# A decoder block in split float32: the slots of the 4 KB tiles made 64 bytes longer

## The chip, the cores and the metric

The kernel runs on one core of one Trainium2 chip. The metric is the device time of one execution in microseconds (us), the median over several runs. Three runs of the kernel before gave 1765.37, 1765.73 and 1765.88 us, so the median is 1765.73 us.

## The reference

One decoder block works on 256 tokens of width 2048 in float32:

```
u    = rmsnorm(x)
proj = u @ w_in                       # 2048 x 16896: HGRN2 q,f,i,gate | attention q,k,v | two merge gates
ya   = hgrn2(...)  @ w_proj_a         # 16 heads of 128, gated linear recurrence
yb   = dilated_attention(...) @ w_proj_b   # 3 groups of 4 heads
mix  = sigmoid(gate_a) * ya + sigmoid(gate_b) * yb
h    = x + mix @ w_out
v    = rmsnorm(h)
hc   = causal_conv3(v @ w_up) + conv_b     # 2048 x 11264
h    = h + (gelu(hc[:, :5632]) * hc[:, 5632:]) @ w_down
out  = rmsnorm(h)
```

Nearly all of the arithmetic lies in the products with the weight matrices. All inputs and outputs are float32.

## The kernel before, in words

**Arithmetic.** The kernel multiplies float32 numbers with the faster float32r matmuls of the TensorE. Each operand is split into a part `hi` (the float32r rounding) and a part `lo` (the rest), and a product is the sum of three matmuls: hi by hi, hi by lo, lo by hi. The weights are split on the chip: ACT writes `hi` (L248), DVE writes `lo` (L249).

**The stream of weights.** All weight matrices are laid out beforehand as one stream of 300 units of 16 tiles (128 x 128). The SP queue loads each unit (1 MB) into a `raw` tile. `split(u)` turns it into two `hi` and two `lo` tiles of 4 KB per partition each, and `next_tiles(n)` (L282) hands out the next n weight tiles of 128 columns. Three units ahead are loaded and two are split. These tiles lie in the pool `wp`, which has three slots of 8 KB for `raw` and four slots of 4 KB each for `hi` and `lo`.

**The two kinds of product step.** `moving_step` (L381) uses four weight tiles as the moving operand of 512 columns. Its stationary operand is a piece of 128 columns of the activations, `xl` or `xh`. It issues three matmuls for each of two token halves: L386 (`xl` by `hi`), L387 (`xh` by `hi`) and L388 (`xh` by `lo`). The stage of the feed-forward block, both merge gates, the two projections and the output product run this way. Counted from the loops there are 976 such steps, so 1952 matmuls at each of the three lines, 5856 in all. `tile_step` (L296) does it the other way round: one weight tile is stationary, and the activations are the moving operand. L299 takes `hi` by 512 columns (both parts of the activations), L300 takes `lo` by 256 columns. There are 56 x 16 = 896 such pairs, for the columns that are wanted transposed.

**Weight loads.** Every matmul is preceded by its own load of the stationary operand (the rows LDWEIGHTS, engine PEld). The load for the next matmul runs beside the matmul before it.

**Tiles and slots.** Almost every other large tile comes from `w4` (L158): 28 slots of 4096 bytes per partition, in the pool `sb`. The split activations `xu`, `hv`, `mix`, `ob`, `ot` and `ff` are `w4` tiles, and so are the inputs, the gates and the state of the recurrence. The pools lie behind each other in the order `const`, `wp`, `sb`, and `w4` is the first tag of `sb`. The slots of `wp` add up to a multiple of 512 bytes, so every `hi`, `lo` and `w4` slot begins at the same place of its 512 bytes, and every piece of 128 columns (512 bytes) does too. In this text the **phase** of an operand is its start minus the start of the `hi` tiles, modulo 512 bytes; it is 0 for all of these. A few smaller tiles have another phase, which follows from the sizes of the tiles in their order, each slot rounded up to 32 bytes: `ones_r` (in `const`, used at L556 and L557) has 416, the tag `o2` with the tiles `ks` (L577) has 384 (twelve slots of 32 bytes lie ahead of it), and `a01` (the `a` of L612) has 320. The tile `z` (L601) is a `w4` tile with phase 0.

**Order of the work.** The products of the weight stream set the order on the TensorE. The recurrence and the attention are written as generators, from which `pump` (L265) takes steps, so their small float32 matmuls and transposes stand between the products (L475 to L632). In the feed-forward block the transposes at L797 do.

Of the kernel before, what the change touches and what calls it, by code (L numbers as in the profile page):

```python
# [13 lines left out]
U8 = mybir.dt.uint8  # L14
# [4 lines left out]
P = 128  # L19
# [128 lines left out]
def hybrid_block(ctx, tc, x_p, x_t, weights, g1, gf, params, c_rope, c_mask0, c_mask1, c_level, out):  # L148
# [5 lines left out]
    sb = ctx.enter_context(tc.tile_pool(name="sb", bufs=1))  # L154
# [1 line left out]
    pss = ctx.enter_context(tc.tile_pool(name="pss", bufs=4, space=bass.MemoryType.PSUM))  # L156

    def w4(shape, name, dt=F32):  # L158
        return sb.tile([P] + list(shape), dt, tag="w4", name=name, bufs=28)

    def w1(name, n=T, dt=F32):
        return sb.tile([P, n], dt, tag="w1", name=name, bufs=12)
# [29 lines left out]
    def in_turn(*instructions):  # L192

        with ExitStack() as stack:
            for i in instructions:
                stack.enter_context(tc.issue_after(i.ins))
            yield

    xt = [w4([4, T], f"xt{q}") for q in range(4)]

    def load_x(k0, k1):
# [19 lines left out]


    xu = [w4([2, 2, T], f"xu{i}", F32R) for i in range(KD // 2)]

    def x_pair(k):
# [114 lines left out]
    def first_norm():  # L340
        for q in range(4):
            sq = w4([4, T], f"sq{q}")
            act.activation(sq, xt[q], AF.Square)
            r = w1("ssqp", T) if q else ssq
            vec.tensor_reduce(r, sq.rearrange("p k t -> p t k"), axis=AX.X, op=ALU.add)
            if q:
                vec.tensor_tensor(ssq, ssq, r, op=ALU.add)
            yield 1.7
        rsqrt_rows(ssq, D, rstd, "rstd1")
        yield 4.0  # L350
        for i in range(2):
            vec.tensor_tensor(rope[:, i], rope[:, i], rstd, op=ALU.mult)
        ps = side_bank("rt")
        for m in range(2):
            pe.transpose(ps[:, m * P : (m + 1) * P], rstd[:, m * P : (m + 1) * P], ident)
        for m in range(2):
            vec.tensor_copy(rst[:, m : m + 1], ps[:, m * P : m * P + 1])
        with in_turn(*last):
            lower_bounds()
        yield 2.0  # L360
# [305 lines left out]
    for g in range(NGRP):  # L666
        z = four(f"z{g}", True)
        f = w4([2, HG, P], f"f{g}")
# [19 lines left out]
    for n in range(2):  # L688
        for j in range(NJ):
            t = w4([2, 512], f"eg{n}_{j}")  # L690
# [46 lines left out]
    for j in range(NJ):  # L737
        t = w4([2, 512], f"h{j}")
# [23 lines left out]
    for j in range(NJ):  # L762
# [4 lines left out]
        for i in range(2):  # L767
            pt = side_bank(f"ht{j}_{i}").rearrange("p (c t) -> p c t", c=2)
            for c in range(2):
                for m in range(2):  # L770
                    n = (2 * i + c) * P
# [123 lines left out]
```

## Time and profile before

| what | value |
|---|---|
| median of three runs | 1765.73 us |
| the profiled execution, its own time | 1768.19 us |
| its span, from first to last instruction | 1766.4 us |
| granted TensorE clock | 0.998 |
| PE busy | 1749.9 us (99%), 8472 matmuls |
| PEld (weight loads) busy | 1463.5 us (83%) |
| DVE busy | 1092.5 us (62%) |
| ACT busy | 888.6 us (50%) |
| read from HBM | 321.41 MB |

PE rows are matmuls. [...] In a timeline row the columns are start, duration, engine, line, operation, out<-in by tile names, and shape. In a row that names a single group, `x352` is the count, and three numbers behind a colon are the shortest, median and longest duration in ns; in rows with a bar, the numbers are the busy time in us and the mean of one in ns, and then the idle time before.

### The profile page before, as it was taken

The page shows a single profiled execution, that of the slowest core. Times are in us where ns is not written, and L with a number is a line of the kernel's source. Part 1 is how long each engine was busy: PE and PEld are TensorE (multiplying, and loading weights), DVE is VectorE, ACT ScalarE, POOL GpSimd, SP SyncE. Part 2 cuts the span into 40 slices and gives each one's busy share as a digit, 9 for nine tenths or more (in the row PEclk, how much of TensorE's full clock was granted, in tenths as well). Part 3 has the DMA queues.
Part 4 walks back from the last instruction along what each step waited for, and adds up shares of the span by engine and source line. Part 5 has one row for each costly group of instructions (what it writes and reads, how often), then busy time and mean ns, then how long its engine had stood idle before and what let it go on. Part 6 is the DMA issues. An engine that isn't in the chain of part 4 may idle for free.

```text
span 1766.4 us, 21297 instructions
## 1 busy us (share of the span) xinstructions
PE 1749.9 (99%) x8472; PEld 1463.5 (83%) x8472; DVE 1092.5 (62%) x1295; ACT 888.6 (50%) x1084; POOL 9.4 (1%) x24
## 2 busy tenths in 40 slices
PE   9999999999999999999999999999999999999997
PEld 7888888888888888888888888888888888888885
DVE  7765575777768675445565556666664456666654
ACT  6444465545454555444445455555543345555442
POOL 0000000000000000000000000000000000000000
PEclk9999999999999999999999999999999999999999
DMA  7665634544444444555556555455555554555552
GB/s 274 220 209 201 228 143 145 179 165 179 167 167 167 166 168 167 191 190 191 191 185 227 185 191 185 177 186 191 182 189 196 196 188 176 184 215 185 188 197 98
DMA packets 48371, 328.02 MB, mean 186 GB/s; under 512 B 5600, under 2 KB 5856, under 8 KB 10128
## 3 DMA queue, kind: packets, MB, share of 16 engines
q1 hardware_dynamic: 45648, 318.28, 50.7%
q0 software_dynamic: 1472, 5.24, 1.1%
q10 hardware_dynamic: 1152, 3.15, 0.5%
q8 instruction: 66, 1.08, 0.2%
q14 instruction: 33, 0.27, 0.0%
HBM read 321.41 MB, written 2.10 MB: 183 GB/s over the span
## 4 chain that ended last, share of the span: by engine, by line
PE 97%; DVE 1%; DMA 1%; ACT 0%; issue 0%; SPq 0%; DVEq 0%; ACTq 0%
PE ub L387 5%; PE ub L386 5%; PE ub L388 5%; PE ua L387 5%; PE ua L388 5%; PE ua L386 5%; PE dn L387 5%; PE dn L386 5%; PE dn L388 5%; PE egp L388 3%; PE egp L386 3%; PE egp L387 3%; PE ak L299 3%; PE aq L299 2%; PE wo L388 2%; PE gp L387 2%
## 5 line engine op out<-in xcount | busy, mean ns | idle before, releaser
L249 DVE TENSOR_TENSOR lo<-raw,hi 128x1024 fp32r<-128x1024 f32 (+1 forms) x602 | 734.5, 1221 | 575.5 <-ACT hi L248 565.9
L248 ACT ACTIVATE hi<-raw 128x1024 fp32r<-128x1024 f32 (+1 forms) x602 | 636.0, 1057 | 763.3 <-PE dn L387 127.3
L387 PE MATMUL ub<-hi,hv 128*128 128x512 f32 x352 | 139.2, 395 | 0.0
L387 PE MATMUL ua<-hi,hv 128*128 128x512 f32 x352 | 138.8, 394 | 0.0
L387 PE MATMUL dn<-hi,ff 128*128 128x512 f32 x352 | 137.4, 390 | 0.0
L386 PE MATMUL ub<-hi,hv 128*128 128x512 f32 x352 | 137.3, 390 | 0.0
L386 PE MATMUL ua<-hi,hv 128*128 128x512 f32 x352 | 137.3, 390 | 0.0
L388 PE MATMUL ub<-lo,hv 128*128 128x512 f32 x352 | 137.2, 390 | 0.0
L388 PE MATMUL ua<-lo,hv 128*128 128x512 f32 x352 | 137.2, 390 | 0.0
L386 PE MATMUL dn<-hi,ff 128*128 128x512 f32 x352 | 137.1, 390 | 0.0
L388 PE MATMUL dn<-lo,ff 128*128 128x512 f32 x352 | 137.1, 389 | 0.0
L386 PE MATMUL egp<-hi,xu 128*128 128x512 f32 x256 | 100.7, 393 | 0.0
L388 PE MATMUL egp<-lo,xu 128*128 128x512 f32 x256 | 99.9, 390 | 0.0
L387 PE MATMUL egp<-hi,xu 128*128 128x512 f32 x256 | 99.8, 390 | 0.0
L386 PEld LDWEIGHTS ub<-hi,hv 128*128 128x128 f32 x352 | 66.1, 188 | 14.0
L386 PEld LDWEIGHTS dn<-hi,ff 128*128 128x128 f32 x352 | 66.1, 188 | 13.8
L386 PEld LDWEIGHTS ua<-hi,hv 128*128 128x128 f32 x352 | 66.1, 188 | 13.8
L388 PEld LDWEIGHTS dn<-lo,ff 128*128 128x128 f32 x352 | 66.1, 188 | 13.6
L387 PEld LDWEIGHTS dn<-hi,ff 128*128 128x128 f32 x352 | 66.1, 188 | 13.5
L388 PEld LDWEIGHTS ua<-lo,hv 128*128 128x128 f32 x352 | 66.2, 188 | 13.1
L387 PEld LDWEIGHTS ua<-hi,hv 128*128 128x128 f32 x352 | 66.2, 188 | 13.0
L388 PEld LDWEIGHTS ub<-lo,hv 128*128 128x128 f32 x352 | 66.2, 188 | 13.0
(435 smaller groups left out, 3154.9 us busy)
## 6 DMA issues: line engine op xcount, KB each, us to landing
raw<-weights SPq DMA_DIRECT2D x298, 1024.0 KB, 4.8
h<-x_t ACTq DMA_DIRECT2D x4, 512.0 KB, 7.5
xt<-x_p SPq DMA_DIRECT2D x3, 512.0 KB, 10.3
xs_q<-aqraw POOLq DMA_DIRECT2D x6, 256.0 KB, 6.8
xs_k<-akraw POOLq DMA_DIRECT2D x6, 256.0 KB, 7.2
raw<-weights SPq DMA_DIRECT2D x4, 256.0 KB, 4.8
raw<-weights SPq DMA_DIRECT2D x2, 512.0 KB, 8.1
gfb<-gf POOLq DMA_DIRECT2D x2, 512.0 KB, 6.6
```

The source lines that it names most:

```text
L248: last[0] = act.activation(hi[:, q * w : (q + 1) * w], raw, AF.Copy)
L249: last[1] = vec.tensor_tensor(lo[:, q * w : (q + 1) * w], raw, hi[:, q * w : (q + 1) * w].bitcast(F32), op=ALU.subtract)
L299: pe.matmul(ps, hi, pair, start=(k == 0), stop=False, skip_group_check=True)
L386: pe.matmul(pst[m], xl, hi, start=(k == k0), stop=False)
L387: pe.matmul(pst[m], xh, hi, start=False, stop=False)
L388: pe.matmul(pst[m], xh, lo, start=False, stop=(k == k0 + nk - 1))
```

## The change

Only the helper `w4` differs. It takes a tile of 4160 bytes per partition, whatever the shape asked for, and returns a view of its first bytes in that shape:

```diff
     def w4(shape, name, dt=F32):
-        return sb.tile([P] + list(shape), dt, tag="w4", name=name, bufs=28)
+
+        n = math.prod(shape)
+        t = sb.tile([P, (4096 + 64) // (1 if dt == U8 else 4)], dt, tag="w4", name=name, bufs=28)[:, :n]
+        names = "abcd"[: len(shape)]
+        return t.rearrange(f"p ({' '.join(names)}) -> p {' '.join(names)}", **dict(zip(names, shape)))
```

Slot number s of `w4` now begins 64 x s bytes later than before, so its phase is 64 x s modulo 512: one slot in eight keeps phase 0, the others take 64, 128, 192, 256, 320, 384 and 448. The slots of `wp` and `const` stay where they are. The 28 slots take 1792 bytes more per partition, so the tags behind `w4` move on by 1792 bytes, which is 256 modulo 512 (`ks` goes from phase 384 to 128). The instructions, their shapes, their order and the waits that the program states are the same.

## Prediction

> **What bounds the kernel now.** I read the page first: the span, the busy times, and the chain that ended last.
>
> ```profile
> span 1766.4 us, 21297 instructions
> PE 1749.9 (99%) x8472; PEld 1463.5 (83%) x8472; DVE 1092.5 (62%) x1295; ACT 888.6 (50%) x1084; POOL 9.4 (1%) x24
> PEclk9999999999999999999999999999999999999999
> PE 97%; DVE 1%; DMA 1%; ACT 0%; issue 0%; SPq 0%; DVEq 0%; ACTq 0%
> ```
>
> The chain is matmuls for 97% of the span, at full clock. Nothing else ends last anywhere that matters, so the time is the number of matmuls times the distance between their starts, and only a change of that distance can move it. The profiled execution took 1768.19 us, 1.8 us more than its span and 2.5 us more than the median of the runs; I add my differences to the median.
>
> Next I took the timeline of a quiet stretch, in the output product, to see that distance.
>
> ```profile
> 1000.50 0.39 PE L387 MATMUL wo<-hi,mix 128*128 128x512 f32 x1
> 1000.73 0.39 PE L388 MATMUL wo<-lo,mix 128*128 128x512 f32 x1
> 1000.73 0.19 PEld L386 LDWEIGHTS wo<-hi,mix 128*128 128x128 f32 x1
> 1000.95 0.39 PE L386 MATMUL wo<-hi,mix 128*128 128x512 f32 x1
> ...
> 1001.86 0.39 PE L387 MATMUL wo<-hi,mix 128*128 128x512 f32 x1
> ```
>
> From 1000.50 to 1001.86 there are six distances, so one is 1.36 / 6 = 0.227 us. The load of the next weights starts with the matmul and lasts 0.19 us, so it lies beside the matmul that streams. The 5856 matmuls of the moving steps cost about 5856 x 0.227 = 1329 us of the span. The pairs of the tile steps look like this:
>
> ```profile
> 121.78 0.40 PE L299 MATMUL ak<-xu,hi 128*128 128x512 f32 x1
> 122.01 0.28 PE L300 MATMUL ak<-xu,lo 128*128 128x256 f32 x1
> ...
> 123.19 0.40 PE L386 MATMUL avp<-hi,xu 128*128 128x512 f32 x1
> ```
>
> Four pairs fit between 121.78 and 123.19, so a pair takes 0.353 us, and the 896 pairs take 316 us.
>
> **What the change can touch.** It adds no instruction, no wait and no byte of transfer. It moves the start of operands. Two reads run together on the TensorE: the moving operand of one matmul and the weights of the next. Before, both begin at phase 0 in every product; after, the activations have phases of 64 x s. The question is what a matmul loses when the weights beside it are read from another phase. The trace of before holds a few such cases, and one where no weights are read beside the matmul at all. The latter is the first matmul of a block, when the transposes behind it wait for ACT.
>
> ```profile
> 1035.31 0.39 PE L386 MATMUL ub<-hi,hv 128*128 128x512 f32 x1
> 1035.57 0.20 PEld L797 LDWEIGHTS ua0t<-ident,ua0u 128*128 128x128 f32 x2 [0.30 <-ACT ua0u L789]
> ...
> L386 PE MATMUL ub<-hi,hv 128*128 128x512 f32 x1 | 0.4, 388 | 0.0
> ...
> L386 PE MATMUL ub<-hi,hv x352: 388/389/398, 1035.3 to 1643.7; 128*128 128x512 f32 x176
> ```
>
> The matmul at 1035.31 has the array to itself: the next load starts 0.26 us later, past the 0.227 us that a matmul takes of the stream. Its duration is 388 ns. The median of its line, with weights of phase 0 read beside it, is 389 ns. So in the kernel before, the load beside the matmul costs 1 ns, 1.5 at most. **This is what there is to win** by taking the two reads apart: 5856 x 1.5 x 7/8 (one slot in eight keeps its phase) = 7.7 us. The shortest duration anywhere gives a wider bound:
>
> ```profile
> L387 PE MATMUL egp<-hi,xu x256: 386/389/398, 623.0 to 808.5; 128*128 128x512 f32 x128
> ```
>
> With 386 in place of 389 and a half for all, the gain would be 3.5 x 7/8 x 5856 = 17.9 us. I take this as the lower end.
>
> The side work gives the cost of other phases. In each of the next groups the line with PEld shows which weights were read beside the matmul of the product, and the row with the bar gives that matmul's own duration. The first is phase 0 (`z`), then 320 (`a`), 384 (`ks`) and 416 (`ones_r`).
>
> ```profile
> 684.46 0.19 PEld L601 LDWEIGHTS lv<-qp,z 128*128 128x128 f32 x1
> ...
> L388 PE MATMUL egp<-lo,xu 128*128 128x512 f32 x1 | 0.4, 388 | 0.0
> ```
> ```profile
> 697.62 0.19 PEld L612 LDWEIGHTS ho<-v,a 128*128 128x128 f32 x1
> ...
> L388 PE MATMUL egp<-lo,xu 128*128 128x512 f32 x1 | 0.4, 389 | 0.0
> ```
> ```profile
> 678.08 0.19 PEld L577 LDWEIGHTS lv<-qp,ks 128*128 128x128 f32 x1
> ...
> L388 PE MATMUL egp<-lo,xu 128*128 128x512 f32 x1 | 0.4, 396 | 0.0
> ```
> ```profile
> 628.20 0.19 PEld L556 LDWEIGHTS dg<-pr,ones_r 128*128 128x128 f32 x1
> ...
> L388 PE MATMUL egp<-lo,xu 128*128 128x512 f32 x1 | 0.4, 397 | 0.0
> ```
>
> Phases 0 and 320 leave the matmul at 388 and 389 ns. Phases 384 and 416 lengthen it to 396 and 397 ns, though the load itself keeps its 0.19 us. The reader is to see that a phase other than 0 never made a matmul shorter by more than the 1 ns, and that some phases cost 7 ns. `z`, `a` and `ks` are plain float32 weights and `ones_r` is float32r, like the products; the kind of number is thus not what divides them.
>
> **The sum.** For the moving steps I take the eight phases as equally frequent. Phase 0 costs nothing, by definition. 320 has its own row, 389 against a mean of 389 or 390 in the lines of the products: I take -1 ns, the most that it can be. 384 has +7 ns. 448 has no row; its nearest is 416, so +7. 64, 128, 192 and 256 have none; 64 lies next to 0, 256 next to 320, and the other two between them, so I take 0 for all four. The sum is (-1 + 7 + 7) / 8 = 1.62 ns per matmul, or 5856 x 1.62 = 9.5 us. The bounds: if the four unknown phases cost 7 ns too, it is (6 x 7 - 1) / 8 = 5.1 ns, or 30 us; if all seven gain, it is the -7.7 or -17.9 us from above.
>
> For the tile steps the roles are turned: the weights stay at phase 0 and the moving operand goes to 64 x s. The same side loads beside them show nothing dearer:
>
> ```profile
> 528.77 0.19 PEld L557 LDWEIGHTS dg<-pr,ones_r 128*128 128x128 f32 x1
> ...
> L299 PE MATMUL z3p<-xu,hi 128*128 128x512 f32 x2 | 0.7, 392 | 0.0
> ...
> L299 PE MATMUL aq<-xu,hi x128: 390/398/404, 78.0 to 167.2; 128*128 128x512 f32 x128
> ```
>
> The two matmuls there have a mean of 392 ns, where the median of the line is 398. The spread of that line, 390 to 404, shows that pairs do wander; 896 times 6 ns either way is 5 us, which both ends of the range can hold. I take 0.
>
> The rest of the change costs nothing, because it is hidden. ACT and DVE read and write `w4` tiles at new phases, but they are busy for 50% and 62%; if each of their instructions took 1% longer, DVE would be busy for 11 us more under a TensorE at 99%, and if that cover were gone, these 11 us would be the price. The loads of the input into `w4` slots are the same bytes in the same pieces. Where the matmuls grow by some ns nothing else becomes late, since all other engines wait for the TensorE.
>
> So the forecast is 1765.73 + 9.5 = **1775.2 us**, slower by 0.5%.
>
> **The rivals.** *The phase does not matter* (this includes that the slots would not really be moved to new phases, for instance by a rounding of their length to 512 bytes). Then the distances stay at 0.227 and 0.353 us and the time at 1765.7, within 3.5 us. For it speaks that a weight load costs a matmul 1 ns before, and that all 512-byte pieces of all slots give the same 389. Against it speak the 396 and 397 ns. In this kernel the two reads would have to be independent of each other. [...]
>
> *The matmuls become shorter.* The reads would collide at phase 0 for the whole of a load, and be free of each other at most of the others. It decides from the point at which the mean over the slots falls below the 389 of now. Taking away what the load costs gives 1765.7 - 7.7 = 1758 us, the shortest duration for all gives 1748. For it speaks that the four phases from 64 to 256 are unseen; against it, that the matmul without any load beside it is no shorter than 388. [...]
>
> *Every unseen phase costs what 384 costs*, or the disturbance of one matmul carries over to the next ones. This gives 1796 us, and is the upper end of the forecast and no case of its own.
>
> **How the numbers follow.** About 0.2%, or 3.5 us, is what a measurement of this kernel can tell from no change. Two rows of four phases show a cost and none a gain, so slower has the larger chance, 0.50. That the phase does not matter, or that costs and small gains cancel, has 0.27. Shorter matmuls have 0.23, because half of the phases are unseen and their mean decides the sign. The range is 1750 to 1796 us: the lower end is the gain by the shortest duration rounded inwards, the upper end the 30 us. If it is slower, the range of that case alone is 1769 to 1796.
>
> **What would show it right or wrong.** In the profile after, the instructions stay at 21297 and the loads at 0.19 us. If I am right, the groups of L386 to L388 split by tile: pieces in slots of phase 384 and 448 have medians near 396, those of 0 and 320 stay at 389, and the distance in a quiet stretch is 0.227 us in some stretches and 0.232 to 0.234 in others. If the phase does not matter, every one of these groups has the median of before. If the groups fall to 386 or below and the distance to 0.224 us or less, the collision was real and I am wrong on the sign. A median that is the same for all phases, but higher than before, would say that the cost is in the change from slot to slot and not in the phase.

## The result, and the profile after

The changed kernel takes 1787.55 us (median of four runs, 1787.22 to 1787.87), the kernel before beside it 1765.81 us (1765.37 to 1766.58). The ratio is 1.0123, 95% interval 1.0105 to 1.0140: slower by 21.7 us. The forecast was slower by 9.5 us, with a range from 1750 to 1796.

The page of the changed kernel has the same rows as before. Its lines are four higher in number, so L390, L391 and L392 are L386, L387 and L388 of before.

```profile
span 1785.5 us, 21297 instructions
PE 1770.2 (99%) x8472; PEld 1465.7 (82%) x8472; DVE 1093.3 (61%) x1295; ACT 888.2 (50%) x1084; POOL 9.4 (1%) x24
PEclk9999999999999999999999999999999999999998
PE 98%; DVE 1%; DMA 0%; SPq 0%; ACT 0%; issue 0%; DVEq 0%
L253 DVE TENSOR_TENSOR lo<-raw,hi 128x1024 fp32r<-128x1024 f32 (+1 forms) x602 | 734.3, 1221 | 594.0 <-ACT hi L252 584.7
L252 ACT ACTIVATE hi<-raw 128x1024 fp32r<-128x1024 f32 (+1 forms) x602 | 635.9, 1056 | 783.9 <-PE dn L391 131.7
```

The reader is to see what has not changed: the count of instructions, the granted clock, the chain of matmuls, and the mean work of one split on DVE (1221 ns, as before) and ACT (1056 ns, 1057 before). PE is busy for 20.3 us more, and the span is 19.1 us longer; that is less than the 21.7 us between the medians, since the profiled execution of the kernel before lay 2.5 us over its median. The matmuls overlap in the records: one of a moving step lasts about 0.39 us, and the next starts 0.23 us behind it; so a matmul is counted here by the distance between two starts, and not by its duration. The starts of the matmuls, taken one by one in both traces, put all of it on the moving steps: the distances from one of their matmuls to the next add up to 1313.1 us before and 1333.5 us after, while the tile steps go from 309.3 to 308.6 us and the rest from 130.5 to 130.3.

The timeline of the changed kernel shows how, in the down-projection. There every activation tile serves twelve matmuls and then gives way to a tile in another slot. By the tiles' addresses, the tile read from 1306.54 on lies at phase 64, and the two from 1317.69 on at phase 256.

```profile
1306.54 0.39 PE L392 MATMUL dn<-lo,ff 128*128 128x512 f32 x1
...
1309.34 0.39 PE L392 MATMUL dn<-lo,ff 128*128 128x512 f32 x1
```
```profile
1317.69 0.40 PE L392 MATMUL dn<-lo,ff 128*128 128x512 f32 x1
...
1319.07 0.39 PE L392 MATMUL dn<-lo,ff 128*128 128x512 f32 x1
...
1320.43 0.39 PE L392 MATMUL dn<-lo,ff 128*128 128x512 f32 x1
```

At phase 64 twelve distances take 2.80 us, 0.233 each. At phase 256 the first six take 1.38 us (0.230) and the next six 1.36 (0.227, as before the change). So the distance depends on the slot, and it needs some matmuls to settle after a change of slot. Over the whole trace, behind a stretch of another phase, the first eight distances at phase 0 or 256 have means between 227.3 and 231.9 ns, and from the ninth on they stand at 226.6 to 226.8 (85 to 111 cases each).

Sorted by phase over the whole trace, the mean distance of the moving steps (without the few over 250 ns, behind side work) is 229.1 ns at 0, 233.1 at 64, 232.4 at 128, 230.5 at 192, 228.3 at 256, 232.8 at 320, 232.3 at 384 and 229.6 at 448, against 227.1 before. Phases that are 256 apart look alike.

### The profile page after: what moved, and what is told of

The parts are those of the page before. It is cut to its first block, busy times and chain, and to the rows that moved or that the text cites. A ratio compares the mean times of both kernels' runs of the same rounds, so it can differ in the third digit from the quotient of the medians.

```text
span 1785.5 us, 21297 instructions
## 1 busy us (share of the span) xinstructions
PE 1770.2 (99%) x8472; PEld 1465.7 (82%) x8472; DVE 1093.3 (61%) x1295; ACT 888.2 (50%) x1084; POOL 9.4 (1%) x24
## 2 busy tenths in 40 slices
DMA packets 48371, 328.02 MB, mean 184 GB/s; under 512 B 5600, under 2 KB 5856, under 8 KB 10128
## 4 chain that ended last, share of the span: by engine, by line
PE 98%; DVE 1%; DMA 0%; SPq 0%; ACT 0%; issue 0%; DVEq 0%
PE ub L391 5%; PE ua L391 5%; PE dn L390 5%; PE dn L391 5%; PE ub L390 5%; PE dn L392 5%; PE ua L390 5%; PE ua L392 5%; PE ub L392 5%; PE egp L390 3%; PE egp L392 3%; PE egp L391 3%; PE ak L303 3%; PE wo L390 2%; PE aq L303 2%; PE wo L392 2%
## 5 line engine op out<-in xcount | busy, mean ns | idle before, releaser
L253 DVE TENSOR_TENSOR lo<-raw,hi 128x1024 fp32r<-128x1024 f32 (+1 forms) x602 | 734.3, 1221 | 594.0 <-ACT hi L252 584.7
L252 ACT ACTIVATE hi<-raw 128x1024 fp32r<-128x1024 f32 (+1 forms) x602 | 635.9, 1056 | 783.9 <-PE dn L391 131.7
L391 PE MATMUL ub<-hi,hv 128*128 128x512 f32 x352 | 140.5, 399 | 0.0
L391 PE MATMUL ua<-hi,hv 128*128 128x512 f32 x352 | 140.2, 398 | 0.0
L391 PE MATMUL dn<-hi,ff 128*128 128x512 f32 x352 | 138.8, 394 | 0.0
L390 PE MATMUL dn<-hi,ff 128*128 128x512 f32 x352 | 138.6, 394 | 0.0
L392 PE MATMUL dn<-lo,ff 128*128 128x512 f32 x352 | 138.5, 393 | 0.0
L390 PE MATMUL ua<-hi,hv 128*128 128x512 f32 x352 | 138.4, 393 | 0.0
L390 PE MATMUL ub<-hi,hv 128*128 128x512 f32 x352 | 138.3, 393 | 0.0
L392 PE MATMUL ua<-lo,hv 128*128 128x512 f32 x352 | 138.1, 392 | 0.0
L392 PE MATMUL ub<-lo,hv 128*128 128x512 f32 x352 | 138.1, 392 | 0.0
L390 PE MATMUL egp<-hi,xu 128*128 128x512 f32 x256 | 101.6, 397 | 0.0
L392 PE MATMUL egp<-lo,xu 128*128 128x512 f32 x256 | 100.8, 394 | 0.0
L391 PE MATMUL egp<-hi,xu 128*128 128x512 f32 x256 | 100.4, 392 | 0.0
L390 PEld LDWEIGHTS ub<-hi,hv 128*128 128x128 f32 x352 | 66.1, 188 | 15.3
L390 PEld LDWEIGHTS dn<-hi,ff 128*128 128x128 f32 x352 | 66.2, 188 | 15.2
L392 PEld LDWEIGHTS dn<-lo,ff 128*128 128x128 f32 x352 | 66.2, 188 | 15.1
L390 PEld LDWEIGHTS ua<-hi,hv 128*128 128x128 f32 x352 | 66.2, 188 | 15.1
L391 PEld LDWEIGHTS dn<-hi,ff 128*128 128x128 f32 x352 | 66.2, 188 | 14.9
L392 PEld LDWEIGHTS ua<-lo,hv 128*128 128x128 f32 x352 | 66.3, 188 | 14.2
L392 PEld LDWEIGHTS ub<-lo,hv 128*128 128x128 f32 x352 | 66.3, 188 | 14.0
L391 PEld LDWEIGHTS ua<-hi,hv 128*128 128x128 f32 x352 | 66.3, 188 | 14.0
```

The lines of the kernel that those rows point to most:

```text
L252: last[0] = act.activation(hi[:, q * w : (q + 1) * w], raw, AF.Copy)
L253: last[1] = vec.tensor_tensor(lo[:, q * w : (q + 1) * w], raw, hi[:, q * w : (q + 1) * w].bitcast(F32), op=ALU.subtract)
L390: pe.matmul(pst[m], xl, hi, start=(k == k0), stop=False)
L391: pe.matmul(pst[m], xh, hi, start=False, stop=False)
L392: pe.matmul(pst[m], xh, lo, start=False, stop=(k == k0 + nk - 1))
```

## The experiments

Theory A was that each phase has its own price per matmul. Its rivals were B, that only the change from slot to slot costs; C, that the place of the stationary operand (here the activations, which the expectations call the weights of a matmul) in its own 512 bytes counts and not its distance from the moving operand; and later D, that the stream falls into one of two fixed steps. All experiments but the last two, w32 and view0, start from the kernel before, and all leave its computation in place. A padding tile ahead of the `w4` slots (still 4096 bytes long) gives all activations the same phase:

```diff
+    sb.tile([P, N // 4], F32, tag="pad", name="pad", bufs=1)
+
     def w4(shape, name, dt=F32):
```

**u64** (N = 64).

> All w4 slots keep 4096 bytes, 64 bytes of padding lie ahead of the first, so that every activation piece has phase 64. Theory A (each phase has its own price per matmul, as the changed kernel shows it by phase: 64 costs 6.0 ns over the 227.1 of before): 5856 x 6.0 = 35 us more, 1801 us, distances near 233 ns everywhere. Theory B (only the change of phase from slot to slot costs, by breaking the even step of the stream): 1766 us, 227 ns. Theory C (what counts is where the weights lie in their 512 bytes, not where they lie against the moving operand): 1801 us as A, and the kernel both64 too.

**u256** (N = 256).

> 256 bytes of padding ahead of the w4 slots, phase 256 everywhere. Theory A: the changed kernel shows 1.2 ns more at this phase, so 5856 x 1.2 = 7 us more, 1773 us. Theory B: 1766 us. Theory C: 1773 us.

**u320** (N = 320).

> 320 bytes of padding ahead of the w4 slots, phase 320 everywhere. Theory A: 5.7 ns more per matmul, 33 us, 1799 us. Theory B: 1766 us. My prediction's own row for 320 (389 ns, no cost) says 1766 us or 6 us less; it was one load after a stretch of phase 0, so it and theory A differ by what a whole stretch of the phase does.

**both64** moves both operands of the moving steps, the `hi` and `lo` tiles and the activations, by the same 64 bytes:

```diff
+    const.tile([P, 16], F32, name="pad")
     g1s = const.tile([P, KD], F32, name="g1s")
```

> 64 bytes of padding at the head of the first pool, so that weights and activations both move by 64 bytes and the phase stays 0. Theories A and B: 1766 us, 227 ns. Theory C: 1801 us.

Measured against 1766.58 us of the kernel before: u64 1802.06 us (ratio 1.0201, 1.0186 to 1.0216), u320 1802.34 (1.0202, 1.0187 to 1.0217), u256 1767.08 (1.0003, 0.9994 to 1.0013), both64 1766.34 (0.9998, 0.9989 to 1.0008). The timelines of the down-projection, six distances each, of u64, u256 and both64 in this order:

```profile
1310.06 0.39 PE L390 MATMUL dn<-lo,ff 128*128 128x512 f32 x1
...
1311.46 0.39 PE L390 MATMUL dn<-lo,ff 128*128 128x512 f32 x1
```
```profile
1299.84 0.39 PE L389 MATMUL dn<-hi,ff 128*128 128x512 f32 x1
...
1301.20 0.39 PE L389 MATMUL dn<-hi,ff 128*128 128x512 f32 x1
```
```profile
1300.08 0.39 PE L387 MATMUL dn<-hi,ff 128*128 128x512 f32 x1
...
1301.44 0.39 PE L387 MATMUL dn<-hi,ff 128*128 128x512 f32 x1
```

They take 1.40, 1.36 and 1.36 us, so 0.233 us per matmul at phase 64 and 0.227 at 256 and 0. B falls: u64 and u320 have one phase throughout and lose more than the changed kernel does. C falls: both64 has the activations at the same new place as u64, but the moving operand moves with them, and it costs nothing. A stands, with a pattern that repeats after 256 bytes (64 equals 320, 256 equals 0). Its 7 us for u256 did not come, though: the 1.2 ns that the changed kernel shows at phase 256 are the settling after a change of slot, and u256 has no such change.

**u128, u192, u32, u224** (N as named) fill in the curve.

> 128 bytes of padding ahead of the w4 slots, phase 128 everywhere. So far phases 64 and 320 cost 36 us alike and phase 256 nothing, so the pattern seems to repeat every 256 bytes. Theory A (each phase has its own price, read from the changed kernel: 5.2 to 5.3 ns at 128 and 384): 31 us more, 1797 us. Theory D (the stream falls into a fixed step that is a whole number of 20/3 ns on average, 34 of them at phase 0 and 35 at 64, and the prices in between that the changed kernel shows are mixtures of the two): either 1766 or 1802 us, nothing between; by the 5.2 ns 1802.

> 192 bytes of padding, phase 192 everywhere. Theory A: 3.4 ns (192) and 2.5 ns (448) in the changed kernel, so 15 to 20 us more, 1781 to 1786 us. Theory D: 1766 us or 1802 us, with steady distances of 226.7 or 233.3 ns.

> 32 bytes of padding, phase 32 everywhere. If the price grows evenly with the distance between 0 and 64: 18 us more, 1784 us. If pieces of 64 bytes are what counts: 1766 us. Theory D: 1766 or 1802 us. If a phase near 0 is better than 0 itself: below 1762 us.

> 224 bytes of padding, phase 224 everywhere, 32 bytes short of the full 256. Even course between 192 and 256: about 8 us more, 1774 us. If the sign of the distance does not matter it is the same as phase 32. Theory D: 1766 or 1802 us.

Measured against 1765.98 us: u128 1798.31 (ratio 1.0179, 1.0164 to 1.0194), u192 1778.78 (1.0071, 1.0054 to 1.0088), u32 1798.00 (1.0179, 1.0164 to 1.0194), u224 1800.09 (1.0192, 1.0177 to 1.0207). D falls with u192, which lies between the two times that D allows. Its timeline:

```profile
1309.98 0.39 PE L390 MATMUL dn<-lo,ff 128*128 128x512 f32 x1
...
1311.36 0.39 PE L390 MATMUL dn<-lo,ff 128*128 128x512 f32 x1
```

Six distances take 1.38 us, 0.230 each. The prices of u128 and u192 are 32.3 and 12.8 us, where A expected 31 and 15 to 20. The even course that the expectations of u32 and u224 offered (18 and 8 us) is wrong: 32 bytes beside phase 0, on either side, nearly the full price is due (32.0 and 34.1 us).

**h16 and h240** look closer at phase 0, and **u96 and u160** (N as named) complete the curve. In the first two the `hi` and `lo` tiles begin 16 or 240 bytes into slots that are 256 bytes longer (here h16):

```diff
-            hi = wp.tile([P, half], F32R, tag="hi", name=f"hi{u}_{s}", bufs=4)
-            lo = wp.tile([P, half], F32R, tag="lo", name=f"lo{u}_{s}", bufs=4)
+            hi = wp.tile([P, half + 64], F32R, tag="hi", name=f"hi{u}_{s}", bufs=4)[:, 4:4 + half]
+            lo = wp.tile([P, half + 64], F32R, tag="lo", name=f"lo{u}_{s}", bufs=4)[:, 4:4 + half]
```

> The hi and lo slots are 256 bytes longer and their tiles begin 16 bytes in, so the activations have phase 240 everywhere, 16 bytes short of the full 256. Theory A with an even course around phase 0 (32 and 224 cost 32 and 34 us): about 1782 us. [...] If some place beside 0 is better than 0: below 1762 us.

> As the kernel h16, with the tiles 240 bytes in, so phase 16 everywhere. Even course: 1782 us; full price from the first 16 bytes on: 1798 us; if weights that lie a little ahead of the moving operand are better than weights at the same place: below 1762 us.

> 96 bytes of padding ahead of the w4 slots, phase 96 everywhere, between 64 (36 us more) and 128 (32 us more). A course without jumps gives 34 us more, 1800 us. Theory D (multiples of 20/3 ns) fell with phase 192 at 229.0 ns per matmul and is not carried on.

> 160 bytes of padding, phase 160 everywhere, between 128 (32 us more) and 192 (13 us more): 23 us more, 1789 us, if the course has no jumps. The prediction's single load at 416, the same place modulo 256, lengthened its matmul from 389 to 397 ns, which would be 1800 us or more.

Measured against 1767.01 us: h16 (phase 240) 1789.02 (ratio 1.0124, 1.0109 to 1.0139), h240 (phase 16) 1815.26 (1.0273, 1.0258 to 1.0289), u96 1806.18 (1.0220, 1.0205 to 1.0236), u160 1798.40 (1.0178, 1.0161 to 1.0195). The timeline of h240 has the largest distance of all, six in 1.42 us, 0.237 each:

```profile
1329.89 0.40 PE L388 MATMUL dn<-lo,ff 128*128 128x512 f32 x1
...
1331.31 0.40 PE L388 MATMUL dn<-lo,ff 128*128 128x512 f32 x1
```

All expectations for 16 and 240 bytes were off: 16 bytes ahead cost 48.3 us, 16 bytes short 22.0. u96 costs 39.2 us where a course without jumps gave 34; u160 costs 31.4 where that course gave 23, and comes out near the 1800 us that the prediction's single load at phase 416 pointed to. None of the nine other places tried is better than 0. The prices at 16 and 240 carry a reservation: in h16 and h240 alone the `hi` and `lo` tiles begin at an odd multiple of 16 bytes, while in all other runs both operands begin at multiples of 32. No run moves both operands by 16 bytes, so a part of these two prices could belong to that place itself. The whole curve, as the difference of the medians of each kernel and of the kernel before beside it:

| phase modulo 256 | 0 | 16 | 32 | 64 | 96 | 128 | 160 | 192 | 224 | 240 |
|---|---|---|---|---|---|---|---|---|---|---|
| us more | 0 | 48.3 | 32.0 | 35.5 | 39.2 | 32.3 | 31.4 | 12.8 | 34.1 | 22.0 |

**w32 and view0** are the changed kernel with another length of the slots:

```diff
-        t = sb.tile([P, (4096 + 64) // (1 if dt == U8 else 4)], dt, tag="w4", name=name, bufs=28)[:, :n]
+        t = sb.tile([P, (4096 + 32) // (1 if dt == U8 else 4)], dt, tag="w4", name=name, bufs=28)[:, :n]
```

and with 4096 alone in view0. They ask whether the curve adds up.

> The changed kernel with slots longer by 32 bytes in place of 64: the slots take all eight phases that are multiples of 32. If the prices of the single phases (0, 32.0, 35.5, 39.2, 32.3, 31.4, 12.8 and 34.1 us for a whole kernel at 0, 32, ... 224) simply add by the share of matmuls in each slot, it is 27.3 us more than before. If going from tile to tile with another phase costs about 4 us on top, as the same sum leaves open in the changed kernel: 31 us more. If mixing phases is cheaper than a whole stretch of one: below 25 us.

> The changed kernel with the tile and view written the new way, but slots of 4096 bytes: all phases 0. Every theory that puts the loss on the phase: no difference from before, within 0.2%. If the rewriting of the helper itself, by other views or other bounds of the tiles, has a part in it: up to the 4 us that the sum leaves open.

Measured against 1766.77 us: w32 1794.35 (ratio 1.0157, 1.0143 to 1.0171), so 27.6 us more, as the sum has it (27.3). view0 1765.89 (0.9996, 0.9987 to 1.0005): the new way of writing the helper has no part in the loss.

For the change itself, the sum by shares goes as follows. Counted by the addresses of the tiles, 26% of the distances of the moving steps belong to phase 0 modulo 256, 19% to 64, 21% to 128 and 34% to 192. That gives 0.19 x 35.5 + 0.21 x 32.3 + 0.34 x 12.8 = 17.9 us of the 21.7. The interval of the ratio, 18.5 to 24.7 us, does not quite reach the sum, and about 4 us are left. The traces show where they lie. Compared with kernels of one phase (227.1 ns in view0, 229.0 in u192), the moving steps of the changed kernel take 228.8 ns on average at 0 and 256, and 230.2 at 192 and 448. Over all such distances this makes 2.5 and 2.3 us more; at the other four phases they are faster by 0.7 us together, which leaves 4.1 us. So in this mixture the cheap phases are dearer than alone. w32 changes slots as often and shows the same: its phases 0 and 192 (modulo 256) take 2.4 us more than alone, the six others 1.4 us less, and only 1.0 us remains. That its sum came out is therefore in part an offset between the two.

## Why the prediction was right in sign and wrong in size

**The bound** held. The chain stayed with the matmuls (98%), and all of the difference is distance between their starts.

**The mechanism and the sign** held. Where the stationary operands lie at another phase than the moving operand, the distance is longer (0.230 us in u192, 0.233 in u64, 0.237 in h240, in place of 0.227), unless the two are 256 bytes apart (0.227 in u256). The rows that gave the sign hold up: 384 and 416 lie modulo 256 at 128 and 160, and u128 and u160 cost 32.3 and 31.4 us. The rival that the phase does not matter is refuted by u64 with 2%: 1802.06 us where 1766.58 should have stayed, and a distance of 0.233 in place of 0.227 us. The rival of shorter matmuls is refuted too: none of the places tried beats phase 0 (u256, the nearest, has 1767.08 us against 1766.58).

**The step that failed** is the sum over the eight phases, with its terms "I take 0 for all four" and "-1 ns" for 320. Spread over the matmuls of the moving steps, the kernels with one phase throughout show 35.5 / 5856 = 6.1 ns at 64 and 320, 5.5 at 128, 2.2 at 192, and nothing at 256; 384 and 448 had no kernel of their own and are taken to cost what 128 and 192 do, since the pattern repeats. The forecast had 0 at 64, 128 and 192, -1 at 320, and 7 at 384 and 448. Its two dear phases were too dear, and four others that cost something were free or a gain; so the errors offset each other in part. The test that the prediction named shows the same: in the changed kernel the median durations by slot are 389 ns at 0 and 256, 394 at 64, 320 and 192, 393 at 128 and 384 and 392 at 448, where 396 was expected at 384 and 448 and 389 at 320. With the measured prices and its own equal shares the sum would have been (35.5 + 32.3 + 12.8) / 4 = 20.2 us, that is 1786 us. That it comes so close to the result is in part luck, since the shares were not equal and the real ones give 17.9 us.

Two things led to these terms. The first is that a phase without a row was given the value of its neighbours, on an even course; the measured curve has none, as 0 and 16 bytes or 192 and 224 show. The second is the gauge. A single load of phase 320 behind a stretch of phase 0 left its matmul at 389 ns, but a whole stretch of it costs 36 us in u320. The trace of the changed kernel shows how both can be true. At 719.36 a slot of phase 320 is loaded for the first time behind slots of phase 0 and 256, at 719.59 for the second time. The first of the two matmuls is recorded with 388 ns, like the prediction's row, the second with 398:

```profile
719.36 0.39 PE L392 MATMUL egp<-lo,xu 128*128 128x512 f32 x1
...
719.59 0.40 PE L390 MATMUL egp<-hi,xu 128*128 128x512 f32 x1
```

Over the 21 such places, with at least eight loads of phase 0 or 256 ahead, the distance beside the first load is 225.9 ns on average, no more than at phase 0, and beside the second 235.9. Where the new phase is 128, already the first is dear (232.5 ns, 30 places). So a single load behind a stretch of phase 0 shows what the first load costs, which is nothing at 320, and not what the next ones cost.

The duration of one matmul is no measure of the distance either. u192 has the same kind of row that the prediction used for a matmul without a load beside it:

```profile
1062.51 0.40 PE L388 MATMUL ua<-hi,hv 128*128 128x512 f32 x1
1062.76 0.20 PEld L799 LDWEIGHTS ub0t<-ident,ub0u 128*128 128x128 f32 x2 [0.29 <-ACT ub0u L791]
...
L388 PE MATMUL ua<-hi,hv 128*128 128x512 f32 x1 | 0.4, 397 | 0.0
...
L388 PE MATMUL ua<-hi,hv x352: 388/394/476, 1016.6 to 1629.8; 128*128 128x512 f32 x176
```

Nothing is loaded beside the matmul at 1062.51 while it streams, and yet it is recorded with 397 ns, over the median of its line. This is no single case: of the 22 matmuls that stand like it ahead of the transposes, all have 388 ns in the kernel before, and 21 have 397 in u192. So the duration changes with the phase even where nothing is loaded beside the matmul; why is open. The 388 ns without a load, from which the prediction took what there is to win, therefore did not show the price of a load. That it gave the right bound (the gain of every phase tried is nil) was luck.

**The tile steps** were put at 0, and 308.6 against 309.3 us agree with it; view0, with all phases at 0, has 307.1, so 2 us either way cannot be told from nothing. **The hidden work** stayed hidden: DVE is busy for 1093.3 us in place of 1092.5.

That the read of the stationary operand and the read of the moving operand hinder each other is the author's reading of both64 and u64 (0.227 and 0.233 us), and it is not shown: no run here has the matmuls of the stream without their loads, and the loads themselves keep their duration, a median of 187 ns at phase 64 and 188 before:

```profile
L388 PEld LDWEIGHTS ua<-hi,hv x352: 187/187/190, 1026.1 to 1650.1; 128*128 128x128 f32 x176
L388 PE MATMUL ua<-hi,hv x352: 393/394/482, 1026.4 to 1650.4; 128*128 128x512 f32 x176
```

## What to carry to other kernels

In a stream of float32r matmuls with 512 columns like this one, keep stationary and moving operands at the same place modulo 256 bytes, which slots whose lengths are multiples of 256 bytes do by themselves as long as what lies between the two pools' starts is such a multiple too; padding them apart cost 0.7 to 2.7% here, and 256 bytes apart cost nothing (1767.08 us against 1766.58). Price such an effect by the distance of starts over a whole stretch, and not by the duration of one instruction, nor by the first of its kind behind a stretch of another kind (here 225.9 ns beside the first load of phase 320, and 235.9 beside the second). Where half of a curve has no row, let the range and not the middle carry it, and do not assume an even course.

## What the runs showed that was not expected

The price of the phase repeats after 256 bytes: 64 and 320 give 1802.06 and 1802.34 us, 0 and 256 give 1766.58 and 1767.08. It is not symmetric: 16 bytes cost 48.3 us, 240 cost 22.0. And the largest price stands next to the place that costs nothing, with the reservation made above for these two. In a mixture of phases the price of a matmul depends on what ran before it: in the changed kernel a return to phase 0 or 256 takes about eight matmuls to become free again (227.3 to 231.9 ns, then 226.6 to 226.8), while behind a settled stretch of these phases the first load at phase 320 is free (225.9 ns) and the second is not (235.9).
